# A list schedule with longer assumed transfers from scratch DRAM, wider margins for short products, and one weight buffer moved from raw to high parts

## The chip, the cores and the metric

One core of one Trainium2 chip runs the whole kernel. The metric is the time of one execution on the device in microseconds, taken as the median of several runs; a profiled execution has its own time, stated beside its span.

## What is computed

One layer of a streaming encoder, 512 tokens wide 1024: a mixer of four parallel branches (Mamba-2, RG-LRU, retention, RWKV-7), then a convolutional feed-forward block, then a final norm. Cut to what matters here:

```python
def hybrid_mixer(h, ...):
    proj = h @ w_in                       # 1024 -> some 15,000 columns
    y_ssd, y_lru, y_ret, y_rwkv = ...     # four token mixers on slices of proj
    branch = einsum('bsmw,mwd->bsmd', stack(ys), w_branch)
    merged = sum(sigmoid(gate_logits) * branch, axis=2)
    return merged @ w_out

def rwkv7_branch(...):                    # per head of 64, over 512 tokens
    def step(state, inp):
        sk = einsum('bhvk,bhk->bhv', state, kk_t)
        state = state * w_t - sk * b_t + v_t * k_t
        return state, einsum('bhvk,bhk->bhv', state, r_t)

def conv_ffn(h, ...):
    u = causal_dwconv(h @ w_up, ...)
    return (silu(gate) * val) @ w_down
```

## The kernel before

All tensors are float32. A weight block is 128 x 1024 values. `wraw` (L450) loads it into a tile `raw`; `wsplit` (L456) has ScalarE cast it to a high part `whi` (L447) and VectorE subtract for a low part `wlo` (L448). Each product of 512 columns is then three matmuls (`mm3`, L465): high by high (L466), low by high (L467), high by low (L468). These write to the accumulators `acc`, three PSUM tiles. They are called long products below; 256- and 272-column ones (L587 to L589) do the same for token-major projections. All other products are short: plain float32, two recorded matmuls each, in the PSUM pools `inn`, `ra` and `rb`.

The RWKV branch runs in chunks of 64 tokens for eight pairs of heads (j = 0 to 7). For each pair there is a preparation (`rwkv_a1`, `rwkv_a2`) and a chain (`rwkv_b`). The preparation ends with a triangular solve on VectorE (L770 to L775), whose result goes through DRAM to change its layout: from `xr` to the scratch tensor `xd` (four DMAs, L781) and from `prod` to `xtd` (four, L782), then back from `xd` to `xr` (two, L787) and from `xtd` to `tt` (four, L790). The chain begins with two groups of 16 tiny products of 32 x 32: L801 needs the new `xr`, L811 needs `tt` and what ScalarE copied out of L801's result. Then, for each of eight chunks, come L824, a copy on VectorE, L828, copies on ScalarE and VectorE, L832, an update on VectorE, and the next chunk's L824. In this text such a pair of groups, L801 and L811, is called a solve, numbered one to eight.

The other mixers (`filler`, L1188) are written in between. Every mixer writes its output to the DRAM scratch tensors `y` (`spill`, L592). The branch stage (`branch`) reads them back into `yr` (L1224), splits them into `yh` and `yl`, and multiplies by the branch weights; a gate product (`proj("gate", ...)`) belongs to every output tile. Its SBUF pool `bp` lies where the mixers' pool `fl` was and opens when that is closed; the emptied gate tile `gt` lies in `bp` too. After the branch stage come the output projection, the feed-forward block and the final norm, nearly all long products.

The order of the code is not the order of issue. At the end of the kernel `_order` (L390) takes all instructions, builds their dependencies and buffers (`_graph`) and runs a list schedule (`_run`) on assumed durations (`_cost`) several times with new priorities (`_latest`); it keeps the run that ends first by its own count and chains the instructions of each engine (TensorE, VectorE, ScalarE, GpSimd, SP) in that order. On TensorE, short products go ahead of long ones once their inputs are assumed to be there for at least a margin (`_MARGIN`, 50 ns); until then long products fill in. A DMA is assumed to hold SP for 450 ns and to land 1500 ns after its bytes have passed. SP issues all transfers of the stages in question, in order; a weight load waits there until its `raw` tile is free.

Of the kernel before, what the change touches and what calls it, by code (L numbers as in the profile page):

```python
# [65 lines left out]
_MARGIN = 50.0  # L66
_RUNS = 12
_HOP = 60.0
_SWITCH = 500.0


def _base(name):
    return name.rsplit("_", 1)[0]
# [73 lines left out]
def _graph(nc):  # L147
# [79 lines left out]
    for p, old in gate.items():  # L227
        gates[p] = [q for q in old if (q in psum) == (p in psum)]
    acc = [i.engine == E.PE and _base(i.outs[0].bass_ap.tensor.name) == "acc" for i in ins]
# [6 lines left out]
def _run(g, prio, margin):  # L236
# [11 lines left out]
    held, table, wire, was = [], "", 0.0, False  # L248
# [8 lines left out]
    def offer(k):  # L257

        for n in g.news[k]:
            if queue[g.tag_of[n]][0] != n or not room[g.tag_of[n]]:  # L260
                return False
            if any(pool_left.get(q, 0) for q in g.gates.get(g.pool_of[n], ())):
                return False
        for n in g.news[k]:
            queue[g.tag_of[n]].pop(0)
            at, old = heapq.heappop(room[g.tag_of[n]])
            est[k] = max(est[k], at)
            if old:
                behind.setdefault(k, []).append(old)
            for q in g.gates.get(g.pool_of[n], ()):  # L270
                est[k] = max(est[k], pool_end.get(q, 0.0))
        heapq.heappush(pend[ins[k].engine], (est[k], k))
        return True
# [18 lines left out]
    while len(seq) < len(real):  # L292
        best = None
        for e in engines:
            if ready[e]:
                t = free[e]
            elif pend[e]:
                t = max(free[e], pend[e][0][0])
            else:
                continue  # L300
            if best is None or t < best[0]:
                best = (t, e)
# [4 lines left out]
        early = []  # L307
        if e == E.PE:
            while ready[e] and not g.acc[ready[e][0][1]] and ready[e][0][0] >= 0 and est[ready[e][0][1]] + margin > t:
                early.append(heapq.heappop(ready[e]))  # L310
            if early and not ready[e]:
                heapq.heapify(early)
                ready[e], early = early, []
        k = heapq.heappop(ready[e])[1]
        for x in early:
            heapq.heappush(ready[e], x)
# [7 lines left out]
        if e == E.PE and g.small[k] != was:  # L324
            was = g.small[k]
            dur += _SWITCH
# [7 lines left out]
        if type(i).__name__ == "InstDMACopy":  # L334
            free[e] = t + (450.0 if e == E.SP else 100.0)
            dur_of[k] = free[e] - t
            wire = max(wire, t + 450.0) + 4.0 * i.outs[0].bass_ap.size() / 330.0
            done[k] = wire + 1500.0
        opened = bool(g.news[k])
        for s in g.succ[k]:  # L340
            left[s] -= 1
            est[s] = max(est[s], t if k in g.after[s] else t + dur if ins[s].engine == e and e != E.SP else done[k])
            if not left[s]:
                if g.news[s]:
                    held.append(s)
                    opened = True
                else:
                    offer(s)
# [13 lines left out]
def _latest(g, r, chained):  # L362
# [13 lines left out]
    for k in reversed(r.seq):  # L376
        e = g.ins[k].engine
# [4 lines left out]
        for s in g.succ[k]:  # L382
            v = min(v, late[s] - (0.0 if k in g.after[s] else r.dur[k] if g.ins[s].engine == e and e != E.SP else whole))
# [6 lines left out]
def _order(tc, nc):  # L390
# [7 lines left out]
    for n in range(_RUNS):  # L398
# [4 lines left out]
        prio = [first[k] if g.ins[k].engine == PE else late[k] for k in range(g.N)]  # L403
# [7 lines left out]
def tile_hybrid_block(ctx, tc, x, wts, wzdt, lora, lruw, cpack, consts, rettab, nfin, out):  # L411
# [38 lines left out]
    def wraw(kind, j):  # L450
        n = 1088 if kind == "zdt" else 1024
        raw = wp.tile([P, 1088], F32, name="raw", bufs=4)
# [3 lines left out]
    def wsplit(raw, n):  # L456
        hi = wp.tile([P, 1088], F32R, name="whi", bufs=3)
# [1071 lines left out]
```

## Time and profile before

| | us |
|---|---|
| median of 3 runs (1598.83 to 1601.36) | 1600.75 |
| the profiled execution | 1597.41 |
| its span | 1595.6 |
| TensorE busy (97%) | 1546.5 |
| VectorE busy (68%) | 1085.2 |
| ScalarE busy (46%) | 733.9 |
| mean granted TensorE clock | 0.98 |

The span is the time from the first to the last recorded instruction of the profiled execution. Busy times of an engine count overlapping instructions once. The granted clock is the share of TensorE's full clock of 2.4 GHz that it was given; it has two levels, 1.0 and 0.5. PE is TensorE, PEld its weight load, DVE VectorE, ACT ScalarE, POOL GpSimd, SP the engine that issues most DMAs.

### The profile page before, as it was taken

How to read it: one execution, taken by the hardware profiler on the slowest of the kernel's cores; microseconds unless marked ns; L12 is line 12 of the kernel's file. 1: busy time of each engine (PE TensorE's matmuls, PEld its weight loads, DVE VectorE, ACT ScalarE, POOL GpSimd, SP SyncE). 2: the span in 40 equal slices, each digit the busy share in tenths (PEclk: the TensorE clock that was granted, in tenths of full speed). 3: DMA queues.
4: the chain of work that ended last, by engine and by line, in shares of the span. 5: the costliest groups of instructions: out<-in, count | busy, mean ns of one | idle time of the engine just before them, and what ended most of it. 6: DMA issues, size and time to landing. Idle time of an engine off the chain costs nothing.

```text
span 1595.6 us, 22214 instructions
## 1 busy us (share of the span) xinstructions
PE 1546.5 (97%) x8324; PEld 1297.7 (81%) x8324; DVE 1085.2 (68%) x2334; ACT 733.9 (46%) x1198; POOL 60.7 (4%) x78
## 2 busy tenths in 40 slices
PE   7999989999999999999999999999999999999998
PEld 6878868887788888977878878888888888888886
DVE  6797888887888897887765966435335666566233
ACT  6653476447754585358422622323224544444123
POOL 0100000000001000001000100000000000000000
PEclk9999999999999998998999999999999999999999
DMA  5243233233143233353442432434232322323321
GB/s 207 81 126 85 79 109 106 80 106 97 54 144 105 69 104 101 97 163 112 153 128 67 148 102 74 149 103 132 95 130 95 106 92 95 104 92 109 102 94 53
DMA packets 108461, 169.46 MB, mean 106 GB/s; under 512 B 54833, under 2 KB 64305, under 8 KB 108353
## 3 DMA queue, kind: packets, MB, share of 16 engines
q1 hardware_dynamic: 107632, 166.92, 33.0%
q8 instruction: 66, 1.08, 0.3%
q10 hardware_dynamic: 720, 1.11, 0.2%
q14 instruction: 43, 0.34, 0.1%
HBM read 150.66 MB, written 15.24 MB: 104 GB/s over the span
## 4 chain that ended last, share of the span: by engine, by line
PE 85%; DVE 7%; DMA 3%; SPq 2%; ACT 1%; issue 1%; DVEq 0%; ACTq 0%
PE acc L467 19%; PE acc L466 19%; PE acc L468 19%; PE acc L1302 3%; PE acc L1303 3%; PE acc L1301 3%; PE rb L824 2%; PE acc L587 1%; PE ra L719 1%; PE acc L588 1%; PE acc L589 1%; PE rb L828 1%; SPq L782 1%; DVE wlo L448 1%; PE inn L443 1%
## 5 line engine op out<-in xcount | busy, mean ns | idle before, releaser
L466 PE MATMUL acc<-hh,whi 128*128 128x512 f32 (+1 forms) x1240 | 496.7, 401 | 6.3 <-DVE pr L611 4.3
L467 PE MATMUL acc<-hh,wlo 128*128 128x512 f32 (+1 forms) x1240 | 495.7, 400 | 0.5 <-DVE wlo L448 0.4
L468 PE MATMUL acc<-hl,whi 128*128 128x512 f32 (+1 forms) x1240 | 493.4, 398 | 0.1
L448 DVE TENSOR_TENSOR wlo<-raw,whi 128x1024 fp32r<-128x1024 f32 x228 | 278.7, 1224 | 206.5 <-ACT whi L447 205.4
L447 ACT CAST whi<-raw 128x1024 fp32r<-128x1024 f32 x228 | 239.1, 1049 | 390.0 <-PE acc L468 210.0
L466 PEld LDWEIGHTS acc<-hh,whi 128*128 128x128 f32 x1240 | 236.5, 191 | 51.3 <-DVE pr L611 5.2
L467 PEld LDWEIGHTS acc<-hh,wlo 128*128 128x128 f32 x1240 | 236.5, 191 | 43.7 <-issue 1.9
L468 PEld LDWEIGHTS acc<-hl,whi 128*128 128x128 f32 x1240 | 236.3, 191 | 42.6 <-issue 1.2
L468 PE MATMUL acc<-yl,whi 128*128 128x512 f32 x256 | 102.6, 401 | 0.0
L466 PE MATMUL acc<-yh,whi 128*128 128x512 f32 x256 | 102.5, 401 | 0.0
L467 PE MATMUL acc<-yh,wlo 128*128 128x512 f32 x256 | 102.2, 399 | 0.0
L587 PE MATMUL acc<-whi,hh 128*128 128x256 f32 (+1 forms) x256 | 78.1, 307 | 0.7 <-DVE sm L906 0.7
L588 PE MATMUL acc<-wlo,hh 128*128 128x256 f32 (+1 forms) x256 | 77.9, 305 | 0.0
L589 PE MATMUL acc<-whi,hl 128*128 128x256 f32 (+1 forms) x256 | 76.9, 301 | 0.0
L1301 PE MATMUL acc<-whi,gh 128*128 128x512 f32 x176 | 69.4, 395 | 0.0
L1303 PE MATMUL acc<-whi,gl 128*128 128x512 f32 x176 | 69.4, 395 | 0.0
L1302 PE MATMUL acc<-wlo,gh 128*128 128x512 f32 x176 | 69.4, 395 | 0.0
L1356 DVE SCALAR_TENSOR_TENSOR fc<-acc,fw,fc 128x511 f32<-128x511 f32 x88 | 65.7, 747 | 4.0 <-ACT fc L1354 2.5
L775 DVE TENSOR_TENSOR xr<-xr,prod 128x60 f32<-128x60 f32 (+24 forms) x248 | 56.9, 229 | 8.1
L468 PEld LDWEIGHTS acc<-yl,whi 128*128 128x128 f32 x256 | 48.6, 190 | 9.6 <-DVE yl L448 0.2
L466 PEld LDWEIGHTS acc<-yh,whi 128*128 128x128 f32 x256 | 48.6, 190 | 9.2
L906 DVE SCALAR_TENSOR_TENSOR sm<-acc,cp,sm 128x511 f32<-128x511 f32 (+2 forms) x72 | 53.6, 745 | 3.6 <-ACT sm L904 2.3
(334 smaller groups left out, 2454.8 us busy)
## 6 DMA issues: line engine op xcount, KB each, us to landing
raw<-in_wts_dram SPq DMA_DIRECT2D x226, 512.0 KB, 3.3
yr<-y SPq DMA_DIRECT2D x32, 256.0 KB, 3.5
y<-sm SPq DMA_DIRECT2D x24, 256.0 KB, 2.2
nt<-nd SPq DMA_DIRECT2D x32, 128.0 KB, 2.7
sm<-acd SPq DMA_DIRECT2D x16, 256.0 KB, 4.1
x<-in_x_dram SPq DMA_DIRECT2D x4, 512.0 KB, 6.2
sm<-sm SPq DMA_DIRECT2D x32, 64.0 KB, 2.0
ym<-bg SPq DMA_DIRECT2D x16, 128.0 KB, 1.8
```

The lines of the kernel that those rows point to most:

```text
L447: nc.scalar.copy(out=hi, in_=src)
L448: nc.vector.tensor_tensor(out=lo, in0=src, in1=hi.bitcast(F32), op=ALU.subtract)
L466: nc.tensor.matmul(ps, wh, xh, start=first, stop=False)
L467: nc.tensor.matmul(ps, wl, xh, start=False, stop=False)
L468: nc.tensor.matmul(ps, wh, xl, start=False, stop=last)
L587: nc.tensor.matmul(o, hh[:, ko, t], wh[:, s], start=ko == 0, stop=False)
L588: nc.tensor.matmul(o, hh[:, ko, t], wl[:, s], start=False, stop=False)
L589: nc.tensor.matmul(o, hl[:, ko, t], wh[:, s], start=False, stop=ko == KT - 1)
L1301: nc.tensor.matmul(ps[i], xh[:, ko, t], w[0][:, s], start=ko == 0, stop=False)
L1302: nc.tensor.matmul(ps[i], xh[:, ko, t], w[1][:, s], start=False, stop=False)
L1303: nc.tensor.matmul(ps[i], xl[:, ko, t], w[0][:, s], start=False, stop=ko == 2 * nblk - 1)
L1356: nc.vector.scalar_tensor_tensor(out=t[:, s:], in0=ps[:, :S - s], scalar=fw[:, o + 2 - s:o + 3 - s], in1=t[:, s:], op0=ALU.mult, op1=ALU.add)
```

## The change

All of it is in the planner, except for two buffer counts.

- The margin for short products goes from 50 to 100 ns, and for the tiny 32-row products to 300 ns. Ready long and short products are now kept in two lists of their own (`weights`, `shorts`), with the same rule of choice.
- A DMA into SBUF from one of the scratch tensors `xd`, `xtd`, `y`, `ym` and `acd` is assumed to land 2500 ns after its bytes have passed, not 1500.
- The first long product behind a short one is assumed to take 17 ns more (`_BACK`).
- Eight trial schedules are made instead of twelve.
- `raw` has 3 buffers instead of 4, `whi` 4 instead of 3.

```diff
-_MARGIN = 50.0
-_RUNS = 12
+_MARGIN = 100.0
+_RUNS = 8
 _HOP = 60.0
 _SWITCH = 500.0
+_BACK = 17.0
...
         if e == E.PE:
-            while ready[e] and not g.acc[ready[e][0][1]] and ready[e][0][0] >= 0 and est[ready[e][0][1]] + margin > t:
-                early.append(heapq.heappop(ready[e]))
...
+            while ready[e]:
+                k = heapq.heappop(ready[e])[1]
+                heapq.heappush(weights if g.acc[k] else shorts, (-1.0 if g.lead.get(k, k) != k else prio[k], k))
+            early = []
+            while shorts and shorts[0][0] >= 0 and est[shorts[0][1]] + (300.0 if g.small[shorts[0][1]] else margin) > t:
+                early.append(heapq.heappop(shorts))
+            if weights and not shorts:
+                k = heapq.heappop(weights)[1]
+            else:
+                if not shorts:
+                    shorts, early = early, []
+                    heapq.heapify(shorts)
+                k = heapq.heappop(shorts)[1]
+            for x in early:
+                heapq.heappush(shorts, x)
...
-        if e == E.PE and g.small[k] != was:
-            was = g.small[k]
-            dur += _SWITCH
+        if e == E.PE:
+            if g.small[k] != was:
+                was = g.small[k]
+                dur += _SWITCH
+            if not run and g.acc[k]:
+                dur += _BACK
+            run = run + 1 if g.acc[k] else 0
...
-            done[k] = wire + 1500.0
+            done[k] = wire + (2500.0 if i.outs[0].bass_ap.tensor.space != bass.MemoryType.DRAM and
+                              _base(i.ins[0].bass_ap.tensor.name) in ("xd", "xtd", "y", "ym", "acd") else 1500.0)
...
-        raw = wp.tile([P, 1088], F32, name="raw", bufs=4)
+        raw = wp.tile([P, 1088], F32, name="raw", bufs=3)
...
-        hi = wp.tile([P, 1088], F32R, name="whi", bufs=3)
+        hi = wp.tile([P, 1088], F32R, name="whi", bufs=4)
```

The numbers of instructions on TensorE stay the same; their order changes nearly everywhere. Lines of the kernel body stand 16 lower after the change (L801 is L817, L811 is L827, L824 is L840, L828 is L844, L832 is L848, L466 is L482). Three places follow.

TensorE, the sixth solve, before: the end of the stretch between its L801 and L811, in which nine long products stand.

```order
L468 MATMUL acc<-hl,whi 128x512
L811 MATMUL rb<-tt,xr 32x32 x16
L824 MATMUL rb<-sv,g 128x64
L466 MATMUL acc<-hh,whi 128x512
L824 MATMUL rb<-sv,g 128x64
```

The same place after; `yh` is the first operand of the branch stage.

```order
L484 MATMUL acc<-hl,whi 128x512
L817 MATMUL rb<-xr,ab 32x32 x16
L827 MATMUL rb<-tt,xr 32x32 x16
L840 MATMUL rb<-sv,g 128x64 x2
L844 MATMUL rb<-nt,tt 128x128
L848 MATMUL rb<-uv,bt 128x128
L482 MATMUL acc<-yh,whi 128x512
```

The long products between the two groups and behind them are gone from here, and the branch stage's first product follows the first chunk of the chain.

TensorE, the seventh solve, before:

```order
L801 MATMUL rb<-xr,ab 32x32 x16
L468 MATMUL acc<-hl,whi 128x512
L466 MATMUL acc<-yh,whi 128x512
L467 MATMUL acc<-yh,wlo 128x512
L811 MATMUL rb<-tt,xr 32x32 x16
L824 MATMUL rb<-sv,g 128x64
```

And after:

```order
L817 MATMUL rb<-xr,ab 32x32 x16
L482 MATMUL acc<-yh,whi 128x512
L483 MATMUL acc<-yh,wlo 128x512
L484 MATMUL acc<-yl,whi 128x512
L482 MATMUL acc<-hh,whi 128x512
L827 MATMUL rb<-tt,xr 32x32 x16
L840 MATMUL rb<-sv,g 128x64
```

Four long products stand between the two groups instead of three.

SP, the transfers of the sixth solve, before (a number behind a name belongs to one of the scratch tensors `y`):

```order
L593 DMA y_4_100<-yu 128x512
L781 DMA xd<-xr 512x1x8 x4
L782 DMA xtd<-prod 256x1x32 x4
L787 DMA xr<-xd 32x8x32 x2
L790 DMA tt<-xtd 32x8x32 x4
L453 DMA raw<-in_wts_dram 128x1024
```

And after:

```order
L609 DMA y_7_87<-sm 128x512
L797 DMA xd<-xr 512x1x8 x4
L798 DMA xtd<-prod 256x1x32 x4
L803 DMA xr<-xd 32x8x32 x2
L469 DMA raw<-in_wts_dram 128x1024 x2
L806 DMA tt<-xtd 32x8x32 x4
```

Two weight loads moved in between the loads of `xr` and `tt`.

## Rows read from the trace of the kernel before

**Rows 1.** The page, part 1: busy us (share of the span) and instructions.

```profile
PE 1546.5 (97%) x8324; PEld 1297.7 (81%) x8324; DVE 1085.2 (68%) x2334; ACT 733.9 (46%) x1198; POOL 60.7 (4%) x78
```

**Rows 2.** TensorE's groups by line: busy us, mean ns | idle us before, releasers.

```profile
L801 PE MATMUL rb<-xr,ab 32*32 32x32 f32 x256 | 10.7, 229 | 9.5 <-DMA xr<-xd 9.4
L811 PE MATMUL rb<-tt,xr 32*32 32x32 f32 x256 | 7.5, 209 | 3.7 <-DMA tt<-xtd 3.1 <-ACT cs L682 0.5
```

**Rows 3.** TensorE's waits by releaser: us in total, times, longest us.

```profile
PE acc L466 <- DVE pr L611: 4.3, 1, 4.3
PE rb L811 <- DMA tt<-xtd: 3.1, 2, 2.6
```

**Rows 4.** Stages at half clock: us, busy us by engine, granted clock, DMA share, GB/s.

```profile
141.20:148.00 6.80, 5.97 (x30) 5.49 (x26) 3.46 (x7) 2.02 (x6) 2.91 (x2) 0.50 0.49 155
219.70:226.50 6.80, 5.44 (x13) 4.28 (x14) 6.38 (x21) 6.70 (x8) 0.00 (x0) 0.50 0.22 85
...
492.80:496.20 3.40, 3.40 (x15) 3.04 (x14) 2.23 (x5) 1.94 (x4) 0.00 (x0) 0.50 0.94 338
608.80:619.10 10.30, 7.89 (x55) 6.99 (x56) 5.56 (x17) 2.91 (x9) 0.00 (x0) 0.50 0.61 189
728.30:741.90 13.60, 13.55 (x98) 11.28 (x99) 6.04 (x20) 10.05 (x16) 0.00 (x0) 0.50 0.36 116
837.50:844.30 6.80, 6.29 (x48) 5.22 (x48) 1.74 (x3) 2.69 (x6) 0.00 (x0) 0.50 0.36 106
sum 57.90, PE 52.23 PEld 45.19 DVE 34.15 ACT 28.50 POOL 2.91; mean PE 6.53 PEld 5.65 DVE 4.27 ACT 3.56 POOL 0.36
```

**Rows 5.** SP's timeline ahead of the sixth solve: start us, us, what.

```profile
720.54 2.59 SPq L781 DMA_DIRECT2D xd<-xr  x4
723.24 2.53 SPq L782 DMA_DIRECT2D xtd<-prod  x4
725.93 0.97 SPq L787 DMA_DIRECT2D xr<-xd  x2
```

**Rows 6.** DMA issues by line: KB each, median us from issue to landing.

```profile
raw<-in_wts_dram SPq DMA_DIRECT2D x226, 512.0 KB, 3.3
yr<-y SPq DMA_DIRECT2D x32, 256.0 KB, 3.5
y<-sm SPq DMA_DIRECT2D x24, 256.0 KB, 2.2
...
xr<-xd SPq DMA_DIRECT2D x16, 32.0 KB, 2.0
```

**Rows 7.** TensorE's timeline, sixth and seventh solve: start us, us, what [idle before].

```profile
727.81 0.28 PE L801 MATMUL rb<-xr,ab 32*32 32x32 f32 x2 [2.48 <-DMA xr<-xd]
728.35 1.12 PE L801 MATMUL rb<-xr,ab 32*32 32x32 f32 x30 [0.27 <-DMA xr<-xd]
...
835.11 0.28 PE L801 MATMUL rb<-xr,ab 32*32 32x32 f32 x2 [1.71 <-DMA xr<-xd]
```

**Rows 8.** TensorE's timeline, the eighth solve and the chain's first chunk.

```profile
949.10 0.28 PE L801 MATMUL rb<-xr,ab 32*32 32x32 f32 x2 [0.79 <-DMA xr<-xd]
950.23 1.09 PE L801 MATMUL rb<-xr,ab 32*32 32x32 f32 x30 [0.86 <-DMA xr<-xd]
951.25 0.50 PE L467 MATMUL acc<-hh,wlo 128*128 128x512 f32 x1
...
954.45 0.38 PE L828 MATMUL rb<-nt,tt 128*128 128x128 f32 x2
954.59 0.48 PE L468 MATMUL acc<-hl,whi 128*128 128x512 f32 x1
954.91 0.40 PE L466 MATMUL acc<-hh,whi 128*128 128x512 f32 x1
955.14 0.39 PE L467 MATMUL acc<-hh,wlo 128*128 128x512 f32 x1
...
955.61 0.38 PE L832 MATMUL rb<-uv,bt 128*128 128x128 f32 x2
```

More of the change, by code (lines that the diff above doesn't have):

```diff
@@ L228, in _graph @@
         gates[p] = [q for q in old if (q in psum) == (p in psum)]
+    eng = [getattr(i, "engine", None) for i in ins]
     acc = [i.engine == E.PE and _base(i.outs[0].bass_ap.tensor.name) == "acc" for i in ins]
@@ L247, in _run @@
     pend, ready, order = {e: [] for e in engines}, {e: [] for e in engines}, {e: [] for e in engines}
-    held, table, wire, was = [], "", 0.0, False
+    held, table, wire, was, run = [], "", 0.0, False, 1
+    weights, shorts = [], []
     queue = {t: list(q) for t, q in g.queue.items()}
@@ L271, in offer @@
                 est[k] = max(est[k], pool_end.get(q, 0.0))
-        heapq.heappush(pend[ins[k].engine], (est[k], k))
+        heapq.heappush(pend[g.eng[k]], (est[k], k))
         return True
@@ L294, in _run @@
         for e in engines:
-            if ready[e]:
+            if ready[e] or (e == E.PE and (weights or shorts)):
                 t = free[e]
@@ L306, in _run @@
             heapq.heappush(ready[e], (-1.0 if g.lead.get(k, k) != k else prio[k], k))
-        early = []
         if e == E.PE:
-            while ready[e] and not g.acc[ready[e][0][1]] and ready[e][0][0] >= 0 and est[ready[e][0][1]] + margin > t:
-                early.append(heapq.heappop(ready[e]))
[L311 to L316, printed above, removed]
+            while ready[e]:
[13 more added lines that the diff above has]
+                heapq.heappush(shorts, x)
+        else:
+            k = heapq.heappop(ready[e])[1]
         i = ins[k]
@@ L341, in _run @@
             left[s] -= 1
-            est[s] = max(est[s], t if k in g.after[s] else t + dur if ins[s].engine == e and e != E.SP else done[k])
+            est[s] = max(est[s], t if k in g.after[s] else t + dur if g.eng[s] == e and e != E.SP else done[k])
             if not left[s]:
@@ L376, in _latest @@
     for k in reversed(r.seq):
-        e = g.ins[k].engine
+        e = g.eng[k]
         whole = r.done[k] - r.start[k]
@@ L382, in _latest @@
         for s in g.succ[k]:
-            v = min(v, late[s] - (0.0 if k in g.after[s] else r.dur[k] if g.ins[s].engine == e and e != E.SP else whole))
+            v = min(v, late[s] - (0.0 if k in g.after[s] else r.dur[k] if g.eng[s] == e and e != E.SP else whole))
         for s in need.get(k, ()):
@@ L402, in _order @@
         late = _latest(g, r, [PE])
-        prio = [first[k] if g.ins[k].engine == PE else late[k] for k in range(g.N)]
+        prio = [first[k] if g.eng[k] == PE else late[k] for k in range(g.N)]
     behind = mybir.DependencyInfo(mybir.DependencyClass.NoSync, mybir.DependencyReason.DATA)
```

## The prediction

> **What bounds the kernel now.** The page's first part comes first: TensorE is busy 1546.5 of 1595.6 us, no other engine is near it [rows 1]. So the bound is TensorE, and a change of order alone can win only three things: time in which TensorE stands idle, time in which its clock is halved, and the price of changing between its kinds of products. The groups by line come next: the two tiny lines of the RWKV solve, L801 and L811 (32x32 products, 18.2 us busy together), have 9.5 and 3.7 us of idle time ahead of them [rows 2]. Their rows name the releasers: the DMAs that bring xr back from the scratch tensor xd, and tt from xtd. All idle time is 1595.6 - 1546.5 = 49.1 us; 13.2 us belong to those two lines, so 35.9 us lie elsewhere, the kernel's start and end included. Within the kernel the longest single wait is 4.3 us, for VectorE to empty an accumulator [rows 3].
>
> The third view is the table by stage of the stretches in which the granted clock was at 0.5, its lower level of 1.2 GHz: eight stretches, 57.9 us, and in them TensorE is 52.2 us busy [rows 4]. At 2.4 GHz the same products would need half, so they cost up to 29 us. Five of the eight begin inside or right behind one of the eight solves (L801, then L811): 6.8 + 3.4 + 10.3 + 13.6 + 6.8 = 40.9 us [rows 4]. The last views are SP's timeline, the transfers' times to landing and TensorE's timeline around three solves [rows 5 to 8].
>
> **The change part by part.** The instructions are the same (4968 long products of 512 columns and all others); their order changes, and two buffer counts.
>
> 1. Longer transfers from fresh scratch tiles, and 300 ns instead of 50 ns of margin for the tiny products. The planner now assumes 1.0 us more for xr and tt, and keeps L801 and L811 back 0.25 us further: 1.25 us together. What it had wrong is visible on SP's queue: four xd issues take 2.59 us, four xtd 2.53, two xr 0.97, together 6.1 us [rows 5]; the planner counts 10 x 0.45 = 4.5 us, 1.6 us too few. The landing itself, 2.0 us in the median [rows 6], it had about right (0.45 + 0.1 + 1.5). Whichever of the two is wrong, a later place on TensorE, with long products put ahead, covers it. Per solve: the idle time ahead of L801 was 2.48 + 0.27, 1.71 and 0.79 + 0.86 us in the three worst [rows 7, 8], 6.1 us; the rest is 9.5 - 6.1 = 3.4 us, of which I let 3 go. Capped at 1.25 in each of the three: 3 x 1.25 + 3 = 6.8 us. Of the 3.7 us ahead of L811 the longest wait, 2.6 us [rows 3], is capped as well: 1.25 + 1.1 = 2.3 us. Together **-9 us**. Bounds: 0, if SP reaches these transfers later by as much (SP works in order, and in the sixth solve two weight transfers now stand between xr and tt where none stood); -13.2, if all of it goes. I take -9, what the shift covers by the rows.
>
> 2. Clock. Where a solve no longer stands between idle stretches, the fall behind it should go. Three solves already pass without one, the eighth with 0.79 + 0.86 us of idle time ahead of it [rows 4, 8], so waiting is not the whole cause. In the new order solves 1, 3, 4, 7 and 8 lie among 512-column products with four long products or their worth between L801 and L811; 2 and 5 lie among 256-column ones; 6 is bare (next item). I let half of the 40.9 us go: 20.4 us at half clock, **-10 us**. Bounds: 0 and -20. The other three stretches (57.9 - 40.9 = 17.0 us) I leave, since the new order has bare places of its own.
>
> 3. The sixth solve. Before, nine long products stand between its L801 and L811, and more behind. After, L801, L811, two L824, L828 and L832 stand with no long product between them: the accumulators hold gate products that can't be emptied before the branch stage's pool opens, and the first branch product needs its y tile back from scratch. So the chain's hops through ScalarE and VectorE lie open. In the eighth solve the same chain, from the end of L801 at 951.25 to L832 at 955.61, takes 4.36 us [rows 8] with ten long products in it; these step by 0.23 us (954.91 to 955.14 [rows 8]) and cover 10 x 0.23 = 2.3 us. Without them the chain is hardly shorter: **+2.3 us**, and with up to 1 us more if y comes later still I take +3. Bounds 0 (y must be waited for in any order) and +7 (the longest wait of another kind, 4.3 us [rows 3], on top of 2.3).
>
> 4. Margin 100 instead of 50 ns for other short products, and other bare places. The new order has a bare L828, L832, L824 in the first solve's chain (six long products stand there in the eighth, 1.4 us) and one run of 16 short products with evictions between them in the third preparation; the old one had such places too, some of them the waits in rows 3. I set these against each other: **0**, bounds -7 and +7, about a fifth of the 35.9 us. The margin itself helps only waits that it outlasts, 0.05 us more than now.
>
> 5. Change price. A short pair alone among long products takes 0.14 us (954.45 to 954.59), and the long product behind it 0.32 instead of 0.23 [rows 8]. The order has 719 places where a long product follows a short one, 686 before: 33 x 0.09 = 3 us above; 0 below, as the pair's own 0.14 + 0.09 is what the planner counts for it anyway. I take **+1 us**, nearer to the lower end.
>
> 6. Buffers: raw 4 to 3, whi 3 to 4. A weight block is 24 long products, 24 x 0.23 = 5.5 us; three raw tiles are 16 us of cover for a landing of 3.3 us [rows 6]. ScalarE may cast one block earlier; VectorE's wlo stays at three. Were that cover gone, SP's queue would hold the spills behind a waiting weight transfer. **0**, bounds -2 (some idle time of ScalarE's casts) and +4.3 (one more wait of the kind in rows 3).
>
> Sum: -9 - 10 + 3 + 0 + 1 + 0 = -15 us. The profiled execution took 1597.4 us, 3.3 below the median of the runs; from the median, 1600.75 - 15 = 1586 us.
>
> **The rivals.**
> - *All falls go.* If waiting is what halves the clock, all five falls go: another -10, and the accumulator wait of 4.3 us with the fall of 6.8 us behind it (219.7 [rows 4]) need not come back, -4.3 - 3.4: 1600.75 - 15 - 17.7 = 1568 at best, 1577 with half of it. For it: the longest stretch, 13.6 us, follows the longest wait, 2.48 us [rows 4, 7]. Against it: 1.65 us ahead of the eighth solve brought no fall. The Trainium skill, "TensorE: Matmul & The Clock Gate", section "What's actually happening", states that the throttled state is the default and that the clock follows how busy the engine has lately been; by that rule alone the falls would go wherever long products now fill the gap. The trace agrees only in part, as the eighth solve shows.
> - *The gaps move.* The planner's times for VectorE and ScalarE are untouched, so every order that it makes misses by about as much somewhere, and what the solves win is paid back elsewhere: within 0.2% of 1600.75. For it: 35.9 us of idle time have many causes. Against it: the largest single cause is named and aimed at.
> - *Slower: the branch stage starts bare.* At the sixth solve TensorE runs out of long products; if y comes back late, the chain of spill and reload (2.2 us for y<-sm, 3.5 us for yr<-y [rows 6]) stands open, +7, with a fall as long as that of the sixth solve before behind it (13.6 us, +6.8), while solves 2 and 5 keep their falls, so that items 1 and 2 together give only -6: 1600.75 + 7 + 6.8 + 1 - 6 = 1610. It decides once that one gap is over about 4 us.
> - *The change doesn't do what it says*: the planner keeps the best of 8 instead of 12 trials by its own estimate, and the buffers matter to nobody; then only the new estimates act, which is the forecast or "the gaps move".
>
> **How the numbers follow.** Forecast (1579 to 1597): 0.44. All falls go (below 1579): 0.18. The gaps move (within 0.2%, 1597.5 to 1604, about what a measurement of this kernel can tell from no change): 0.15. Slower: 0.23. So faster 0.62, same 0.15, slower 0.23. The range leaves out a tenth on each side: half of the large gain, and the part of the slower case near and beyond its worked price: 1573 to 1608.
>
> **What would show it.** Right: the idle time ahead of L801 and L811 (L817 and L827 after) falls from 13.2 to about 4 us, the stretches at half clock from 57.9 to under 40 us, and a bare stretch of 3 to 4 us stands where the branch products begin. Wrong: those waits stay, or VectorE and ScalarE appear as releasers of new waits over 2 us in the first 950 us, or the half-clock time does not follow the waits. Behind 950 us nothing should change by more than 2 us.

## The result and the profile after

The changed kernel takes 1571.98 us (median of 4 runs, 1569.53 to 1573.08) beside 1599.79 us for the kernel before on the same chip: a ratio of 0.983, interval 0.9805 to 0.985. The forecast was 1586 us: the direction was right, and the gain of 28 us is nearly twice the one forecast (15 us). The time falls just under the low end of the range (1573 us), where the rival "All falls go" stood (1568 to 1577 us).

The page's first part, as [rows 1]:

```profile
PE 1532.9 (98%) x8324; PEld 1286.6 (82%) x8324; DVE 1086.4 (69%) x2334; ACT 734.9 (47%) x1198; POOL 62.9 (4%) x78
```

TensorE's two tiny lines, as [rows 2] (L817 and L827 are the old L801 and L811):

```profile
L817 PE MATMUL rb<-xr,ab 32*32 32x32 f32 x256 | 10.1, 229 | 2.0 <-DMA xr<-xd 1.7
L827 PE MATMUL rb<-tt,xr 32*32 32x32 f32 x256 | 7.1, 203 | 5.2 <-DMA tt<-xtd 4.8
```

The stretches at half clock, as [rows 4], within the kernel (the one that reaches its end left out): start:end, us, busy us by engine (PE, PEld, DVE, ACT, POOL), granted clock, DMA share, GB/s.

```profile
430.90:434.30 3.40, 3.40 (x17) 3.30 (x16) 2.38 (x3) 2.72 (x6) 0.00 (x0) 0.50 0.69 219
622.10:632.30 10.20, 9.52 (x68) 8.77 (x67) 6.29 (x14) 1.97 (x7) 0.00 (x0) 0.50 0.61 187
738.10:748.40 10.30, 7.26 (x51) 6.18 (x52) 3.04 (x8) 5.00 (x10) 0.00 (x0) 0.50 0.59 202
936.10:939.50 3.40, 3.40 (x12) 2.92 (x13) 0.29 (x1) 0.91 (x3) 0.00 (x0) 0.50 0.18 70
sum 27.30, PE 23.57 PEld 21.16 DVE 12.00 ACT 10.61 POOL 0.00; mean PE 5.89 PEld 5.29 DVE 3.00 ACT 2.65 POOL 0.00
```

The span of the profiled execution fell by 24.3 us (1595.6 to 1571.3). Two readings add up to about that. Idle time of TensorE fell from 49.1 to 1571.3 - 1532.9 = 38.4 us, by 10.7, of which the two tiny lines give 13.2 - 7.2 = 6.0. TensorE's busy time at the half clock fell from 52.2 to 23.6 us; half of the difference, 14.3 us, is saved. 10.7 + 14.3 = 25.0. Of the forecast's own signs, the half-clock stretches (27.3 us, under 40) and the bare stretch came; the waits ahead of the tiny lines fell to 7.2 us, not to about 4.

The sixth solve, now bare as the third item said. TensorE's timeline (start us, us, what, [idle before <- releaser]), then SP's queue:

```profile
734.08 1.42 PE L817 MATMUL rb<-xr,ab 32*32 32x32 f32 x32
738.71 1.22 PE L827 MATMUL rb<-tt,xr 32*32 32x32 f32 x32 [3.21 <-DMA tt<-xtd]
739.86 1.11 PE L840 MATMUL rb<-sv,g 128*128 128x64 f32 x4
742.76 0.80 PE L844 MATMUL rb<-nt,tt 128*128 128x128 f32 x2 [1.78 <-ACT tt L830]
744.20 0.76 PE L848 MATMUL rb<-uv,bt 128*128 128x128 f32 x2 [0.65 <-DVE uv L846]
744.62 0.77 PE L482 MATMUL acc<-yh,whi 128*128 128x512 f32 x1
```

```profile
731.86 0.98 SPq L803 DMA_DIRECT2D xr<-xd  x2
732.89 0.92 SPq L469 DMA_DIRECT2D raw<-in_wts_dram  x2
733.98 1.80 SPq L806 DMA_DIRECT2D tt<-xtd  x4
735.90 0.85 SPq L609 DMA_DIRECT2D y<-sm  x2
```

3.21 + 1.78 + 0.65 = 5.6 us stand idle there and tt is issued behind two raw blocks. The half clock sets in at 738.1, within the first of these waits, and lasts to 748.4. That is one place; the gain lies in many others.

The row that the prediction had no term for is the cast's. ScalarE's cast of a weight block (busy us, mean ns | idle us before it, releasers) in the kernel before:

```profile
L447 ACT CAST whi<-raw 128x1024 fp32r<-128x1024 f32 x228 | 239.1, 1049 | 390.0 <-PE acc L468 210.0 <-PE acc L1303 90.1 <-issue 77.5
```

and after:

```profile
L463 ACT CAST whi<-raw 128x1024 fp32r<-128x1024 f32 x228 | 238.1, 1046 | 230.6 <-PE acc L1319 84.7 <-issue 64.2 <-PE acc L484 53.1
```

With three high parts ScalarE stood 210 us in front of a cast, in its queue, until TensorE had used up a high part (L468, after: L484); with four, 53 us. Whatever stands behind such a cast in ScalarE's order, a chain's eviction (the copy that empties an accumulator) for one, waits with it. Most of the 210 us cost TensorE little, though: 143 us of them lie behind 950 us. The same row and VectorE's subtraction for the low part, within the first 950 us alone, before and after:

```profile
L447 ACT CAST whi<-raw 128x1024 fp32r<-128x1024 f32 (+1 forms) x118 | 123.5, 1048 | 100.7 <-PE acc L468 66.6 <-issue 22.0 <-PE acc L589 10.3
L463 ACT CAST whi<-raw 128x1024 fp32r<-128x1024 f32 (+1 forms) x122 | 127.3, 1047 | 74.2 <-PE acc L484 39.7 <-DMA raw<-in_wts_dram 19.2 <-issue 7.9
L448 DVE TENSOR_TENSOR wlo<-raw,whi 128x1024 fp32r<-128x1024 f32 (+1 forms) x118 | 144.1, 1225 | 16.0 <-ACT whi L447 15.2
L464 DVE TENSOR_TENSOR wlo<-raw,whi 128x1024 fp32r<-128x1024 f32 (+1 forms) x121 | 147.6, 1224 | 27.4 <-PE acc L483 16.5 <-PE acc L604 3.6 <-DMA xtd<-prod 2.9
```

So where the chains are, the wait for a free high part falls by 27 us only, waits for raw blocks come in (19.2 us), and VectorE now waits for a free low part instead of for the cast.

TensorE's own idle time by stretch, before, then after (stretch length less PE busy): 14.1, 26.9 and 1.7 us, then 12.3, 19.2 and 0.4 us.

```profile
0.00:100.00 100.00, 85.93 (x498) 74.51 (x499) 76.50 (x185) 61.24 (x98) 8.10 (x14) 1.00 0.41 138
100.00:960.00 860.00, 833.07 (x4973) 704.34 (x4972) 695.20 (x1717) 453.56 (x802) 52.61 (x64) 0.97 0.35 106
960.00:1589.10 629.10, 627.42 (x2857) 518.81 (x2855) 311.31 (x429) 217.46 (x295) 0.00 (x0) 1.00 0.30 102
0.00:100.00 100.00, 87.69 (x514) 76.83 (x515) 77.77 (x183) 64.58 (x103) 8.88 (x15) 1.00 0.42 141
100.00:960.00 860.00, 840.78 (x5067) 709.33 (x5065) 706.29 (x1740) 455.92 (x806) 53.97 (x63) 0.98 0.35 107
960.00:1564.80 604.80, 604.38 (x2749) 500.42 (x2747) 300.16 (x407) 212.71 (x286) 0.00 (x0) 1.00 0.31 103
```

### The profile page after: what moved, and what is told of

It reads as the page before. It is cut to its first block, busy times and chain, and to the rows that moved or that the text cites. A ratio compares the mean times of both kernels' runs of the same rounds, so it can differ in the third digit from the quotient of the medians.

```text
span 1571.3 us, 22179 instructions
## 1 busy us (share of the span) xinstructions
PE 1532.9 (98%) x8324; PEld 1286.6 (82%) x8324; DVE 1086.4 (69%) x2334; ACT 734.9 (47%) x1198; POOL 62.9 (4%) x78
## 4 chain that ended last, share of the span: by engine, by line
PE 83%; DVE 8%; ACT 3%; DMA 3%; SPq 2%; issue 1%; DVEq 0%; ACTq 0%
PE acc L482 19%; PE acc L484 19%; PE acc L483 19%; PE acc L1319 4%; PE acc L1318 4%; PE acc L1317 4%; PE acc L603 2%; PE acc L604 2%; PE acc L605 2%; PE rb L840 1%; PE ra L735 1%; DVE wlo L464 1%; PE rb L844 1%; PE inn L459 1%; PE ra L459 1%
## 5 line engine op out<-in xcount | busy, mean ns | idle before, releaser
L482 PE MATMUL acc<-hh,whi 128*128 128x512 f32 (+1 forms) x1240 | 493.5, 398 | 2.8 <-ACT hh L527 1.8
L484 PE MATMUL acc<-hl,whi 128*128 128x512 f32 (+1 forms) x1240 | 490.4, 396 | 0.0
L482 PEld LDWEIGHTS acc<-hh,whi 128*128 128x128 f32 x1240 | 234.6, 189 | 46.6 <-ACT hh L527 2.5
L484 PEld LDWEIGHTS acc<-hl,whi 128*128 128x128 f32 x1240 | 234.0, 189 | 42.4 <-issue 1.4
L482 PE MATMUL acc<-yh,whi 128*128 128x512 f32 x256 | 103.3, 403 | 0.0
L484 PE MATMUL acc<-yl,whi 128*128 128x512 f32 x256 | 102.4, 401 | 0.0
L1370 ACT ACTIVATE fc<-acc,fw 128x512 f32<-128x512 f32 x44 | 34.4, 782 | 93.2 <-PE acc L484 93.2
L789 DVE TENSOR_TENSOR prod<-nt,xr 128x60 f32<-128x60 f32 (+24 forms) x248 | 53.7, 217 | 5.1 <-DMA nt<-nd 1.9
L484 PEld LDWEIGHTS acc<-yl,whi 128*128 128x128 f32 x256 | 48.7, 190 | 9.8 <-DVE yl L464 0.2
```

What stands on the lines that cost most here:

```text
L482: nc.tensor.matmul(ps, wh, xh, start=first, stop=False)
L484: nc.tensor.matmul(ps, wh, xl, start=False, stop=last)
```

## The experiments

All ratios are to the kernel before, run on the same chip. "Idle" is span less TensorE's busy time, "half" TensorE's busy time at the half clock inside the kernel, "solves" the idle time ahead of the two tiny lines, all us of one profiled execution, while the ratio is of 4 to 10 executions. That execution lay up to 6 us from its kernel's median, furthest in e1 and e6 (6 us over) and in e4 and e14 (4 us under).

| run | ratio (interval) | idle | half | solves |
|---|---|---|---|---|
| before | 1 | 49.1 | 52.2 | 13.2 |
| after | 0.983 (0.9805 to 0.985) | 38.4 | 23.6 | 7.2 |
| e1 solves later by hand | 1.011 (1.008 to 1.013) | 66.9 | 70.5 | 7.7 |
| e2 before, waits filled | 0.994 (0.992 to 0.995) | 43.9 | 28.8 | 5.6 |
| e3 after, SP queue reordered | 0.984 (0.982 to 0.986) | 39.5 | 19.2 | 10.4 |
| e4 after, transfers 1500 ns | 0.992 (0.990 to 0.993) | 43.0 | 41.3 | 9.1 |
| e5 after, old margins | 0.982 (0.9795 to 0.985) | 38.3 | 19.0 | 6.0 |
| e6 after, no 17 ns | 0.990 (0.9875 to 0.993) | 50.8 | 40.2 | 9.9 |
| e7 after, old buffers | 0.9885 (0.986 to 0.991) | 49.3 | 19.6 | 3.1 |
| e8 before, transfers alone | 0.996 (0.995 to 0.997) | 53.3 | 35.1 | 10.8 |
| e9 after, waits filled | 0.982 (0.980 to 0.983) | 36.1 | 17.1 | 5.0 |
| e10 after, transfers 3000 ns | 0.985 (0.9825 to 0.988) | 43.2 | 11.6 | 3.7 |
| e11 after, hop 65 ns | 0.983 (0.981 to 0.985) | 44.8 | 27.7 | 5.1 |
| e12 before, hop 65 ns | 1.004 (1.0025 to 1.005) | 57.6 | 54.0 | 12.6 |
| e13 before, 17 ns alone | 1.004 (1.0025 to 1.006) | 54.9 | 45.8 | 13.6 |
| e14 before, buffers alone | 0.995 (0.993 to 0.997) | 50.6 | 33.3 | 13.0 |
| e15 after, hop 55 ns | 0.990 (0.987 to 0.992) | 47.8 | 21.5 | 2.8 |
| e16 before, hop 55 ns | 1.000 (0.9985 to 1.001) | 54.7 | 37.6 | 13.5 |
| e17 after, 3 raw and 3 high | 0.990 (0.9855 to 0.994) | 52.3 | 20.8 | 5.4 |
| e18 after, 2 raw, 4 high, 4 low | 0.986 (0.983 to 0.990) | 45.1 | 26.7 | 7.3 |

Span less idle less half of "half" is 1516 to 1526 us in every row (e2 and e9 less their 10.7 and 5.0 us of fillers): before 1595.6 - 49.1 - 26.1 = 1520.4, after 1571.3 - 38.4 - 11.8 = 1521.1. So the rest, the price of changing between kinds of products with it, differs by 10 us at most over all rows and by 0.7 us between before and after; idle time and the clock decide.

**e1: the solves later, by hand.** After the planner is done, long products are pulled ahead of each solve in TensorE's order alone.

```diff
+_LATER = (3, 6, 6, 6, 6, 3, 6, 6)
...
+    for p, n in zip(solves, _LATER):
...
+        longs = [k for k in part if g.acc[k]]
+        new, rest = longs[:n], iter(longs[n:])
...
+    _shift(g, best.order[PE])
```

> The kernel before, its own order, with one thing done by hand: 6 long products (3 at the first and the sixth solve) that stood behind a solve are put ahead of it, so that every solve begins some 1.4 us (0.7 us) of TensorE work later. Nothing else of the change is in it. Theory A (the solves stood too early for their transfers, and the waits bring the clock down): of the 9.5 us of idle time ahead of L801 about 6 go (1.0, 1.2, 0.8, 0.7, 1.4 and 0.9 at the third to the eighth solve), and the falls behind the fourth and seventh solve with them (half of 3.4 and of 6.8 us): 6 to 11 us under the kernel before. Theory B (the gain of the change comes from its wholly other order, and a later place of the solves alone does little): within 3 us of the kernel before. Theory C (the short and tiny products bring the clock down by themselves, waits or not): idle time falls by 6 us and every fall stays, 4 to 6 us under it.

Measured: 17 us slower. The wait aimed at did go, 9.5 to 3.7 us ahead of L801, but others came. TensorE's waits by releaser (us in total, times, longest), where L613, L614 and L492 are long products:

```profile
PE acc L613 <- DVE sm L932: 8.2, 2, 4.7
PE acc L492 <- ACT sm L975: 2.9, 1, 2.9
PE inn L1171 <- DVE sm L1157: 2.8, 1, 2.8
PE acc L614 <- DVE wlo L474: 1.7, 1, 1.7
```

The long products now reach accumulators that VectorE or ScalarE hasn't emptied (L613, L492), as these engines keep the order planned for the old places, and the chains' own products come later. Theory A was right on the wait and wrong on the time: here, with the other engines not planned around it, a later place did not pay.

**e2: the waits filled.** The order of before; TensorE gets useless products where it sat idle.

```diff
+_FILL1 = (0, 0, 4, 6, 4, 18, 14, 10)
+_FILL2 = (0, 0, 0, 0, 18, 0, 4, 0)
...
+            _FILLERS.append(nc.tensor.matmul(ps[:, 256:512], hh[:, 0, 0:P], hh[:, 0, 0:256], start=True, stop=True).ins)
```

> The kernel before, its own order, with useless 256-column products that nobody reads put on TensorE where it sat idle ahead of the tiny products: 0, 0, 4, 6, 4, 18, 14 and 10 of them ahead of L801 at the eight solves, 18 ahead of L811 at the fifth and 4 at the seventh. No wait is taken away: TensorE only isn't idle in it. Theory A (idle time ahead of a solve brings the clock down): the falls at 492.8, 608.8, 728.3 and 837.5 go, 34.1 us at the half clock, worth up to 17 us; with some of the fillers in the way of real work 8 to 17 us under the kernel before. Theory C (the tiny and short products themselves bring it down): the falls stay, and the fillers cost 0 to 4 us.

Measured: 0.994, 9 us under before by the medians, though TensorE does 10.7 us more. The mean granted clock is 0.988 to 0.990 in all four executions, beside 0.978 to 0.982 in the seven of the kernel before. Stages of e2 (columns as above), at the places of the old falls at 492.8, 608.8, 728.3 and 837.5:

```profile
492.40:499.10 6.70, 6.70 (x55) 6.08 (x56) 2.91 (x5) 3.68 (x8) 0.00 (x0) 0.50 0.65 248
608.00:618.00 10.00, 9.47 (x108) 8.57 (x103) 5.98 (x19) 3.99 (x12) 0.00 (x0) 1.00 0.82 253
727.90:731.20 3.30, 3.30 (x9) 2.52 (x8) 1.56 (x4) 3.23 (x7) 0.00 (x0) 0.50 0.79 239
836.00:843.00 7.00, 7.00 (x40) 5.96 (x39) 3.59 (x10) 1.47 (x3) 0.00 (x0) 1.00 0.20 73
```

Two of the four falls are gone, the longest is 3.4 instead of 13.6 us. So at these three places idle TensorE brought the fall or its length, as theory A has it, and not the tiny products, which are the same. It doesn't hold everywhere: at the fourth solve 1.50 us of waiting are left ahead of L801 in spite of six fillers (1.22 us before), and the fall there is 6.8 instead of 3.4 us long, with TensorE busy all through it; and the eighth solve, which had no fall before, has one of 3.4 us (946.3). The cause of these two stays open.

**e3: SP's queue at the bare solve.** y are the places of the two spills, x those of xr, t of tt, r of the raw blocks.

```diff
+    sp[x:y[1] + 1] = [sp[i] for i in y + [x, x + 1] + t + r] + [sp[i] for i in range(t[3] + 1, y[1]) if i not in y]
```

> The kernel after, with SyncE's queue alone in another order at the bare sixth solve: the two y spills that stood behind the group come first, then xr, then the four tt loads, then the two raw weight blocks. In the kernel after L827 waits 3.2 us there for tt, L844 1.8 us, and the half clock lasts 10.2 us. Theory A (the row of transfers on SyncE sets that solve): tt lands 1.5 to 2 us earlier, the branch stage behind it begins 1 to 3 us earlier, and with the clock 2 to 6 us are gained on the kernel after. Rival: the raw blocks, 1.8 us later, are waited for instead, or the y spills push xr: within 2 us of the kernel after, or up to 4 us slower than it.

Measured: the same as after. tt is there sooner, and another wait takes its place. TensorE's timeline in e3, then SP's, then ScalarE's:

```profile
738.97 1.45 PE L836 MATMUL rb<-tt,xr 32*32 32x32 f32 x32 [4.56 <-ACT xr L830]
```

```profile
731.77 1.86 SPq L815 DMA_DIRECT2D tt<-xtd  x4
733.69 1.39 SPq L478 DMA_DIRECT2D raw<-in_wts_dram  x3
```

```profile
737.49 1.04 ACT L472 CAST whi<-raw 128x1024 fp32r<-128x1024 f32 x1 [5.57 <-DMA raw<-in_wts_dram]
738.56 0.75 ACT L830 COPY xr<-rb 32x256 f32<-32x256 f32 x2
```

The eviction of xr (L830) stands behind a cast in ScalarE's order; the cast waits 5.57 us for the raw block that was put back, and the solve with it. This is the clearest sight of what a waiting cast does to a chain; the cast waits for a raw block here, not for a free high part.

**e4 to e8: parts undone, and the transfers alone.** Each puts one part back to its old value; e8 does so with all parts but the transfers:

```diff
e4, e8 (e8 the other way)
-            done[k] = wire + (2500.0 if i.outs[0].bass_ap.tensor.space != bass.MemoryType.DRAM and
-                              _base(i.ins[0].bass_ap.tensor.name) in ("xd", "xtd", "y", "ym", "acd") else 1500.0)
+            done[k] = wire + 1500.0
e5
-_MARGIN = 100.0
+_MARGIN = 50.0
...
-            while shorts and shorts[0][0] >= 0 and est[shorts[0][1]] + (300.0 if g.small[shorts[0][1]] else margin) > t:
+            while shorts and shorts[0][0] >= 0 and est[shorts[0][1]] + margin > t:
e6
-_BACK = 17.0
+_BACK = 0.0
e7
-        raw = wp.tile([P, 1088], F32, name="raw", bufs=3)
+        raw = wp.tile([P, 1088], F32, name="raw", bufs=4)
...
-        hi = wp.tile([P, 1088], F32R, name="whi", bufs=4)
+        hi = wp.tile([P, 1088], F32R, name="whi", bufs=3)
```

e8, and e13 and e14 below, keep the eight trials and the two lists of the kernel after. These two alone give the order of the kernel before, instruction by instruction, so each of the three is the kernel before with one part.

> The kernel after with one part undone: the planner counts 1500 ns for every transfer again. Theory A (the longer transfers place the solves right, and this is the larger part of the gain): 10 to 25 us of the 28 us come back, 1582 to 1597 us, with idle time ahead of L817 of 6 us or more and falls of the clock behind solves. Theory B (any order of this planner's new rules would do; the transfers are one part among several): 1568 to 1580 us.

Measured: 1586.8 us, 15 us back, as theory A said: 6.3 of the 9.1 us are waits for xr again, and the half-clock time rises to 41.3 us.

> The kernel after with one part undone: the margin for short products is 50 ns again, the tiny ones' 300 ns too. Theory A (the transfers place the solves; the margins shift a solve by less than 0.3 us): 1570 to 1578 us, idle time ahead of L817 up to 4 us. Theory B (each part of the change is half of a row of reorderings, and any of them undone gives another order with its own luck): 1576 to 1592 us, with the difference in places that have nothing to do with the solves.

Measured: 1571.3 us, no different from after. Theory A.

> The kernel after with one part undone: the 17 ns charged on the first long product behind short ones. By the prediction's fifth item it costs or saves about 1 us: 1569 to 1577 us. Theory B (any other order has its own luck): 1576 to 1592 us.

Measured: 1583.5 us. Theory B, or the 17 ns are worth 11 us; e13 below bears on it.

> The kernel after with one part undone: four buffers for raw blocks and three for their high parts, as before. The sixth item of the prediction put this at nothing, between a gain of 2 and a loss of 4.3 us: 1568 to 1577 us, with the waits of ScalarE for whi going back from 231 towards 390 us and TensorE's own idle time the same. Rival: the fourth high part is what took the 4.3 us wait of the accumulator group at 219 us away: that wait and the fall of the clock behind it come back, 1577 to 1583 us.

Measured: 1582.4 us, 10 us back. Neither expectation: the rival has the time, but not the place, since the accumulator's wait came back only in two pieces (3.2 us) and the fall of the clock there did not. Idle time rises by 10.9 us, in several places, and ScalarE's cast waits as before the change (73 us of this within the first 950 us), in e7:

```profile
ACT whi L463 <- PE acc L484: 222.9, 77, 6.5
```

> The kernel before with one part of the change alone: 2500 ns for transfers from fresh DRAM tiles. Theory A (this part holds most of the gain): 1574 to 1588 us, idle time ahead of L801's products down from 9.5 to under 5 us, two to four falls of the clock behind solves fewer. Theory B (it needs the other parts, or is luck): 1590 to 1606 us.

Measured: 1593.7 us, 6 us faster, theory B. The waits for xr shrink to 2.2 us, but those for tt grow, in e8 (as [rows 2]):

```profile
L817 PE MATMUL rb<-xr,ab 32*32 32x32 f32 x256 | 10.4, 229 | 2.4 <-DMA xr<-xd 2.2
L827 PE MATMUL rb<-tt,xr 32*32 32x32 f32 x256 | 7.6, 203 | 8.4 <-DMA tt<-xtd 8.0
```

**e9: the waits of after filled.** The third row stands ahead of the first L844 of the branch stage.

```diff
+_FILL1 = (0, 0, 0, 0, 6, 0, 0, 0)
+_FILL2 = (0, 0, 0, 0, 0, 20, 0, 0)
+_FILL3 = (0, 0, 0, 0, 0, 10, 0, 0)
```

> The kernel after, its own order, with useless 256-column products that nobody reads in three waits: 6 ahead of L817 at the fifth solve, and at the bare sixth solve 20 ahead of L827 and 10 ahead of the first L844. Theory A (idle TensorE ahead of the tiny products brings the clock down): the falls at 622 and 738 (10.2 us each) go, worth half of the some 18 us that TensorE is busy in them, less what the fillers overrun the waits: 3 to 9 us under the kernel after. Rival (the tiny and short products themselves, or the row of waits in the branch stage that stays): at least one of the two falls stays as long, within 2 us of the kernel after or up to 3 us slower.

Measured: 0.982, not to be told from after. At the sixth solve the clock stays whole; at the fifth the fall is still there, 6.7 instead of 10.2 us long:

```profile
625.00:631.70 6.70, 6.70 (x30) 6.36 (x30) 5.27 (x12) 0.58 (x2) 0.00 (x0) 0.50 0.56 189
736.00:746.30 10.30, 7.62 (x74) 6.39 (x73) 4.06 (x8) 6.28 (x13) 0.76 (x1) 1.00 0.76 216
```

The half-clock time falls by 6.5 us, worth 3.3, and a new short fall came at 833. The time is the rival's, and of the two falls one went and one was shortened. Theory A is borne out on the cause at the sixth solve and too high on the price: the whole clock through the bare solve brought nothing measurable, so there the chain of transfers and evictions seems to set the time.

**e10: a longer estimate still.** 3000 instead of 2500 ns.

> The kernel after with 3000 ns instead of 2500 ns for the transfers from fresh DRAM tiles. Theory A (the estimate places the solves, and tt still came late by up to 3.2 us with 2500): idle time ahead of L827 falls from 5.2 to under 3 us and one or two falls more go: 1562 to 1572 us. Theory B (the length of the estimate hardly matters beside the reordering it sets off): idle ahead of L817 and L827 may fall, and the time is anywhere from 1568 to 1592 us with the difference elsewhere.

Measured: 1577.6 us, theory B. No fall stands behind a solve any more but the first (half 11.6 us), and idle time is 4.8 us more than in after (43.2), 8.3 us more outside the solves. The clock is paid for with waits.

**e11, e12, e15, e16: the width of luck.** `_HOP` from 60.0 to 65.0 or 55.0, on both kernels.

> The kernel after with a number of the planner that the change doesn't touch: the hop between engines is 65 ns instead of 60. Five nanoseconds say nothing of the chip; they only set off another order of the same kind. Theory A (the gain belongs to what the change tells the planner): within 5 us of the kernel after, 1567 to 1577 us. Theory B (each order has its own luck, of some 10 us): over 5 us away from it, most likely slower, 1577 to 1592 us.

> The kernel before with the hop between engines at 65 ns instead of 60. Theory A: within 5 us of the kernel before, 1595 to 1605 us. Theory B (each order has its own luck): over 5 us away from it, to either side; under 1590 us, much of the difference between before and after would be luck as well.

> The kernel after with the hop between engines at 55 ns instead of 60: a second order of no meaning, for the width of luck. With the 65 ns run at 1575.6 us, theory A (luck is under 5 us, so that the 10 to 15 us of the parts undone are theirs): 1567 to 1577 us. Theory B (luck reaches 10 us, and a single part undone can't be told from it): 1577 to 1592 us.

> The kernel before with the hop between engines at 55 ns instead of 60. With the 65 ns run 6 us over the kernel before: theory A (luck is some 6 us), 1594 to 1607 us; theory B (the kernel before was an unlucky order, and a lucky one of the old planner comes near the kernel after), under 1590 us.

Measured: on after 1575.6 and 1583.7 us, on before 1607.6 and 1599.7 us. Five nanoseconds that say nothing of the chip move the time by up to 12 us: e11 within theory A, e12 just past it, e15 theory B, e16 theory A. In e15 the waits ahead of the solves are the lowest of all, 2.8 us, and the time is lost in two other waits (TensorE's, e15):

```profile
PE rb L459 <- DVE rst L1040: 6.5, 1, 6.5
PE rb L844 <- ACT tt L830: 4.5, 2, 3.6
```

The second of them is e3's sight again: the copy that it waits for stands behind a cast that waits for a raw block (ScalarE's timeline, e15).

```profile
151.55 1.04 ACT L463 CAST whi<-raw 128x1024 fp32r<-128x1024 f32 x1 [4.60 <-DMA raw<-in_wts_dram]
152.62 0.74 ACT L830 COPY tt<-rb 32x256 f32<-32x256 f32 x2
```

**e13, e14: the other parts alone on before.**

> The kernel before with one part alone: the 17 ns charged on the first long product behind short ones. Taking it out of the kernel after cost 11 us. Theory A (it is worth some 10 us wherever it stands): 1588 to 1594 us. Theory B (17 ns are as little as the hop's 5 ns: it only sets off another order, and what it was worth in the kernel after was that order): 1595 to 1608 us, the spread of the hop's run.

Measured: 1607.0 us, 7 us slower: theory B. What the 17 ns seemed worth in after (e6) was one order against another.

> The kernel before with one part alone: three buffers for raw blocks and four for their high parts. Undoing it in the kernel after cost 10 us, in idle time of TensorE alone. Theory A (the fourth high part is worth it in any order): 1587 to 1594 us, with idle time 8 to 12 us lower and the 4.3 us wait for pr gone. Theory B (only another order): 1595 to 1608 us.

Measured: 1594.6 us, 0.995: at the edge between both theories. Idle time does not fall, as theory A wanted, but is 1.5 us higher than before (50.6); the half-clock time falls by 19 us, with the solves' waits untouched (13.0). By itself this run doesn't decide; the groups below go further.

**e17, e18: which buffer.** e17 puts high parts back to 3 with 3 raw; e18 takes raw to 2 and low parts to 4.

> The kernel after with the high parts back at three buffers and the raw blocks left at three, so that only the taking away of a raw buffer is left of that part. Theory A (the fourth high part is what pays: it takes the 210 to 230 us of waiting for whi out of ScalarE's queue): the waits of ScalarE for L484's products come back with over 200 us, 1580 to 1590 us. Theory B (it is not the high part but another order, or fewer raw blocks): those waits come back and the time stays at 1571 to 1579 us.

Measured: 1586.2 us, theory A: idle 52.3 us, and in e17

```profile
ACT whi L463 <- PE acc L484: 202.1, 79, 6.4
```

So the waits come back with three high parts, with three raw blocks as with four, and taking a raw block away is not what removes them. The time alone, within the width of luck, would not say so.

> The kernel after with one more buffer moved in the same way: two for raw blocks, four for high and four for low parts. In the kernel after the wait for a free buffer lies on VectorE (157 to 165 us for L483's products, wlo). Theory A (an engine that waits for a buffer holds up the chains queued behind it): VectorE's wait goes too, idle time of TensorE 38 to 30 us, 1560 to 1570 us. Rival (with two raw blocks the raw transfers come late and the wait moves to ScalarE as a wait for raw): 1572 to 1590 us, with waits for raw in place of those for wlo.

Measured: 1582.3 us, the rival's time. VectorE's waits for a free low part are gone, as theory A wanted, but ScalarE waits longer, for raw (21.1 us in after) and for high parts (53.1):

```profile
ACT whi L463 <- PE acc L484: 75.7, 26, 7.1
ACT whi L463 <- DMA raw<-in_wts_dram: 34.6, 20, 5.3
```

**The orders of the planner together.** No single run tells a part of 10 us from luck of 12. In groups by the two parts that matter, mean ratios (idle, half); e18, with two raw blocks, and e1, e2, e3 and e9, which alter an order by hand, are left out:

| | 3 high parts | 4 high parts |
|---|---|---|
| 1500 ns | 1.002 (54.1, 47.4): before, e12, e13, e16 | 0.9935 (46.8, 37.3): e4, e14 |
| 2500 or 3000 ns | 0.9915 (51.6, 25.2): e7, e8, e17 | 0.986 (43.9, 23.9): after, e5, e6, e10, e11, e15 |

The transfers bring 0.0105 and 0.008, mean 0.009 x 1600 = 15 us, most of it clock (half 47.4 to 25.2 and 37.3 to 23.9). The fourth high part brings 0.0085 and 0.006, mean 12 us, most of it idle time (7 to 8 us). Together some 26 us. These are estimates from 15 orders with 2 to 6 in a cell. Taking the spread within the cells (0.003) for luck, each of the two has a standard error of some 3 us and a 95% interval of some 6 us to either side: both gains are clear of zero, but 15 and 12 us can't be told apart. The idle share of the fourth high part has an interval of 5 us to either side. The margins and the 17 ns don't stand out of the spread. No run has four high parts beside four raw blocks, so what is called the fourth high part here always stands with three raw blocks; e17 has three raw blocks alone and is no faster for it.

Where the fourth high part lowers idle time is told by the same stretches as in the result: by 1.5 and 2.4 us (the two rows) in the first 100 us, by 3.8 in both between 100 and 960 us, and by 2.0 and 1.6 behind that. The last is beyond luck: 1.6 to 3.2 us in each of the seven orders with three high parts, 0.3 to 0.6 in each of the eight with four.

## Why the forecast was half of the gain

1. *Transfers, -9.* The waits ahead of the solves fell by 6.0 us in the profile after, and between groups by some 5 to 7: two thirds of the forecast. But idle time as a whole fell by under 3 us between these groups (54.1 to 51.6, 46.8 to 43.9), so about half came back as other waits, as "The gaps move" has it. In e10 and e15 the solves' waits fell further and the time rose. The step's thought that a later place on TensorE by itself covers the wait held for the wait in e1 and not for the time, 17 us more.
2. *Clock, -10.* Measured 14.3 us. The half that I let go was too little, and the 17.0 us of other stretches that I left alone changed as well. e2 shows the mechanism at three solves. The rival "All falls go" was nearer: it has the time, and the 4.3 us accumulator wait of [rows 3] with its fall (it set in at 219.7, during that wait and not behind it) is gone; yet falls stay at the fifth and sixth solve and a short one came behind the eighth. The Trainium skill, "TensorE: Matmul & The Clock Gate", section "What's actually happening", has the clock follow how busy the engine has lately been; e2 and e9 agree at three places, where the fillers stand and the clock is 1.00 instead of 0.50, but not at the fourth and eighth solve of e2.
3. *The bare sixth solve, +3.* The stretch was foreseen and stands: 5.6 us idle and half the clock. The waits sum up to more than the term and lay inside its bounds; e3 and e9 couldn't win them back.
4. *Other margins and bare places, 0, and 5. change price, +1.* e5 (no difference) bears out the margins. The price is in the 1516 to 1526 us that hardly move; bounded rightly.
6. *Buffers, 0, bounds -2 and +4.3.* **This is the step that failed.** I priced the raw block that is taken away and gave the fourth high part no price beyond "ScalarE may cast one block earlier" and 2 us. It is worth about 12 us by the groups, with a low end of about 5; in single runs 8 (e14), 9 (e7) and 11 (e17), by their ratios. What I had not asked is what stands in ScalarE's order behind a cast that waits for a free high part: 66.6 us of such waits before and 39.7 after within the first 950 us. The answer on raw blocks was wrong too. With three of them and four high parts ScalarE waits for raw in every order, 2.9 to 21.1 us (under 1 us with three high parts), in spite of the 16 us of cover, and in e3 and e15 TensorE waits with it.

Items 1 to 3 sum to -16, and the transfers bring about 15. That is partly luck, as the shares are others: by the groups under 3 us of idle time and 7 to 11 of clock. Item 6 is the missing 12. Of the rest, before and after each lie within the spread of their cells, after at its faster end (0.982 to 0.990).

That ScalarE's freed queue is what lowers the idle time is argued, not shown. The waits for a free high part go with the number of high parts in every order (202 to 233 us with three, 38 to 57 with four), and e3 and e15 show a waiting cast that holds up a chain, though for raw. But which evictions gained was not followed one by one, VectorE's waits for the low part grew meanwhile, and most of the 210 us lie where TensorE idled under 2 us. Whether the planner was wrong on SP's issue time or on the landing was not tried apart.

## What to carry to other kernels

An engine that works in order and waits for a buffer holds up all that is queued behind it, so ask of a low busy share what stands behind its waits, and in which stretch: a long wait where the bounding engine never idles is worth little. A buffer moved to where such a wait lies can be worth nearly as much as a better schedule, and can move the wait to the tile that gave it up. Where a planner sets the order, change a number that means nothing and see how far the time moves before a part is credited with a gain, and judge parts in groups of orders. Before one step of a chain is moved to a later place by hand, ask what the other engines, planned around its old place, will do.

## What was not expected of the hardware

Products that nobody reads made the kernel before faster: 78 of them, 10.7 us of TensorE's time, for 9 us less in all, as the granted clock stayed at 1.00 at two places where it had fallen to 0.50 and was low for a shorter time at a third. And the wait ahead of a fall need not be the solve's own: in e1 the sixth solve's L827 begins without any idle time ahead of it, but 0.9 us after the end of a long product's wait of 2.91 us (744.94 to 747.85), and the half clock follows as in the kernel before. TensorE is then busy throughout, and the clock stays low for 13.6 us:

```profile
748.80:762.40 13.60, 13.60 (x102) 11.27 (x102) 5.18 (x20) 9.12 (x16) 0.00 (x0) 0.50 0.34 112
```
